# Other columns of the input projection emitted between the units of the second layer's recurrence

## The chip, the cores and the metric

One core of one Trainium2 chip runs the whole kernel in one launch. The metric is device time in microseconds. The kernel before took 1895.92 us, the median of three runs (1895.07, 1895.92 and 1908.12). All arithmetic is in float32. The large matrix products are done as three products each: both operands are split into a high part (float32r) and a low part, and high x high, high x low and low x high are added up in PSUM.

## The reference

Two layers act on 256 context tokens and 256 latent tokens of width 1024. Each layer starts with one input projection of the modulated stream, whose columns feed all branches:

```
p = modulate(x, shift, scale) @ w_in[l]
cq, ckv, kr, ch, cb, cc, rw, gt = split(p)
A) attention from cq, ckv, kr (low-rank, RMS norm, rotary key)
B) y = cb * conv3(cc * ch)
C) RWKV-7 from rw: features r, k, v, g, kk, decay, a, k_dir,
   then for each direction a scan over the tokens
   S = S*w - (S kk) (kk*a)^T + v k^T;   y = S r
   context first, the latent scan starts from the context's state
gates = sigmoid(gt)
o = (gates_A*(A @ w_o_attn) + gates_B*(B @ w_o_conv) + gates_C*(C @ w_o_rwkv)) @ w_out
x = layer_norm(alpha*x + g1*o)
x = layer_norm(alpha*x + g2*swiglu(modulate(x)))
```

In the second (last) layer only the latent tokens are wanted at the end. There the gates, the convolution, the queries and the read-out are computed for 256 tokens, while what the latent tokens read of the context (k, v, decay and the like, the key and value compression) is computed for 512.

## The kernel before, in words

**Columns.** `w_in` is padded and cut into 57 column blocks of 128 features. One block is `gemm_in` (line 426): 8 steps over the width with three matmuls each (`mm3`, lines 238 to 240), 24 matmuls into one PSUM bank of the pool `psg`, which has two. A block's weights come through a ring of four `hi` and four `lo` buffers of 512 columns, two of each to a block. They are split from the raw weight by ScalarE (`hi`, line 193) and by VectorE or POOL (`lo`, line 194), or, for 35 blocks of layer 1, they have been split during layer 0's FFN, stored in DRAM, and are read back by four DMAs (`wready`, line 209). Those 35 are all recurrence features that are loaded this way, the six compressed blocks, four gates and the twelve convolution blocks. The other 20 gates are split on the spot.

**What is made of a block.** A recurrence feature (`feature`, line 463) is mixed with its neighbours in time and stored to DRAM. A compressed block (line 548) is stored, and its squares are summed by four or two small matmuls (line 559). A gate (line 572) goes through a tanh and is stored. A convolution (`conv`, line 578) takes three blocks. All of them use one tag of four staging buffers (`stage`). Between gates and convolutions `mod_step` computes pieces of the next modulation, one step at a time (line 259).

**Recurrence.** `rwkv_half` (line 947) is a generator that runs once for the context half and once for the latent half of the tokens. Up to its first `yield` it makes eight units, one for each pair of heads and each direction: `stage1` (features, decay, cumulated sums) and `stage2` (products in chunks of 64 into `AR` and `LB`), with `stage1` one unit ahead. After the `yield` it inverts the triangular blocks: 31 steps on VectorE (lines 1085 to 1097), then small matmuls (lines 1110 and 1122). Last comes the scan, four chunks in each direction (lines 1154 to 1213). The latent half of layer 1 also reads out (`y`), and stores the result at line 1215.

**Order.** In layer 1 the program emits: the features except `late_f` (r for four blocks and the output gate's feature), both parts of the context half, the five `late_f`, both parts of the latent half, the six compressed blocks and their inverse norms, four gates, four convolutions, twenty gates. The framework sorts this at build time: each instruction has the rank of its place in the program, and each engine is given, along a simulated time line, the lowest-ranked of those that are ready. On the chip each engine, and SP's DMA queue, then runs its list in order.

**After the mixer.** Attention follows (lines 662 to 770): it loads the compressed blocks, normalizes them with `rsd` (lines 675 to 688) into `ch` and `cl`, and makes v, k and q. `qT` and `kT` are allocated in the space of `xh` and `xl`, the modulated stream that `gemm_in` reads (line 699). `rwkv_tail` (line 1217) finishes the read-out.

Of the kernel before, what the change touches and what calls it, by code (L numbers as in the profile page):

```python
# [12 lines left out]
ALU = mybir.AluOpType  # L13
# [5 lines left out]
T = 512  # L19
HT = 256  # L20
# [4 lines left out]
C = 64  # L25
# [3 lines left out]
RMS_EPS = 1e-6  # L29
# [31 lines left out]
CONV_AT = (20, 4)  # L61
# [7 lines left out]
VB = 1  # L69
# [2 lines left out]

N_AHEAD = 35
AHEAD_W13, AHEAD_W2 = 1.0, 1.0


@with_exitstack
def body(ctx: ExitStack, tc: tile.TileContext, A: dict, out: bass.AP, dbg=None, upto=None):
# [250 lines left out]
    def pow_mhalf(out_, in_, n):  # L329
        e = mhalf[0:out_.shape[0]]  # L330
        for _ in out_.shape[2:]:
            e = e.unsqueeze(2)
        e = e.to_broadcast(list(out_.shape))
        pool.tensor_tensor(out=out_, in0=in_, in1=e, op=ALU.pow)  # L334
# [98 lines left out]
    def seg(a):  # L433
        return a.rearrange("p (s t) -> p s t", t=HT)

    def layer(l, xh=None, xl=None, pre=()):
# [16 lines left out]
        with ExitStack() as rws:  # L453
# [5 lines left out]
            def rt(name, shape, dt=F32, bufs=1):  # L459
                return rp.tile(shape, dt, tag=name, name=name, bufs=bufs)  # L460
# [52 lines left out]
            def feat_gemm(m):  # L513
                feature(m, pre[m - R_K] if 0 <= m - R_K < len(pre) else gemm_in(l, M_RW + m, xh, xl, HT if m in late_f else 0, T))
# [12 lines left out]
                if n == (n0 if last else n0 + 2):  # L527
                    rnT = norms_t(nst["rn"], rt)

            S = [None, None]  # L530
            for z in range(2):
                S[z] = rt(f"S{z}", [128, 4, C])
                pool.memset(S[z], 0.0)
            for half in range(2):
                g = rwkv_half(l, half, last, rt, S, rnT)
                next(g)
                if l == 0 and half == 0:
                    for m in range(R_V, R_GD):
                        v = rt("vin", [128, 2, HT], bufs=VB)
                        sp.dma_start(out=v, in_=seg(feat_d[l][m]))  # L540
                        by_token(m, v, rt("vou", [128, T], bufs=VB))
                next(g, None)
                if half == 0:
                    for m in late_f:
                        feat_gemm(m)


            for i in range(6):
                a = s0 if i < 3 else 0
                ps = gemm_in(l, M_CQ + i, xh, xl, a * HT, T)  # L550
                t = stage("cqs")
                act.copy(out=t[:, a:2, 0:HT], in_=seg(ps)[:, a:2])
                sp.dma_start(out=seg(cq_d[l][i])[:, a:2], in_=t[:, a:2, 0:HT])
                if i < 5:
                    sq = stage("sqs")
                    act.activation(out=sq[:, a:2, 0:HT], in_=t[:, a:2, 0:HT], func=ACTF.Square)
                    pst = pg()
                    for tt in range(2 * a, 4):
                        pe.matmul(pst[:, tt:tt + 1], sq[:, tt // 2, (tt % 2) * 128:(tt % 2 + 1) * 128], ones[:, 0:1],
                                  start=(tt == 2 * a), stop=True, skip_group_check=True)  # L560
                    act.copy(out=ssq[:, i, 2 * a:4], in_=pst[:, 2 * a:4])

            o = q0 // 128
            for i, c, n in ((0, 0, 384), (3, 4, 256)):
                k = o if i == 0 else 0
                r = rsd[:, c + k:c + 4]
                dve.tensor_tensor(out=r, in0=ssq[:, i, k:4], in1=ssq[:, i + 1, k:4], op=ALU.add)
                if i == 0:
                    dve.tensor_tensor(out=r, in0=r, in1=ssq[:, 2, k:4], op=ALU.add)
                dve.tensor_scalar(out=r, in0=r, scalar1=1.0 / n, scalar2=RMS_EPS, op0=ALU.mult, op1=ALU.add)  # L570
            pow_mhalf(rsd[:, o:8], rsd[:, o:8], 8 - o)
            def gate(i):
                ps = gemm_in(l, M_GT + i, xh, xl, q0, T)
                gt = stage("gt")
# [19 lines left out]
                sp.dma_start(out=seg(br_d[l][1][i])[:, s0:2], in_=h_)  # L594


            n = 0
            for i in list(range(8, 24)) + list(range(8)):
                if n == CONV_AT[l]:
                    for k in range(4):  # L600
                        conv(k)
                gate(i)
                if n < N_EARLY[l]:
                    mod_step()
                n += 1
            if CONV_AT[l] > 23:
                for k in range(4):
                    conv(k)
            mod_step(100)
        if upto == "rwkv":  # L610
            mix.close()
# [332 lines left out]
        dve.tensor_copy(out=rnT, in_=prt)  # L944
        return rnT

    def rwkv_half(l, half, last, rt, S, rnT):
        read = not (last and half == 0)
        h0 = half * HT
        ncol = 128 if read else 64  # L950
# [123 lines left out]
        for n, u in enumerate(units):  # L1074
            cur = nxt
            if n + 1 < len(units):
                nxt = stage1(*units[n + 1])
            stage2(*u, *cur)

        yield  # L1080

# [313 lines left out]
```

## Time and profile before

| | |
|---|---|
| median of three runs | 1895.92 us |
| profiled execution | 1895.05 us |
| its span, first to last instruction | 1893.3 us |
| mean granted TensorE clock | 0.972 of full speed |
| TensorE busy, matmuls | 1811.6 us (96%) |
| TensorE busy, weight loads | 1480.6 us (78%) |
| VectorE, ScalarE, POOL busy | 1101.3, 830.8, 584.0 us |
| DMA | 374.16 MB, mean 198 GB/s |

The profiled execution lies 0.9 us under the median. Busy times of engines overlap, so they don't add up to the span. A matmul's busy time contains the time in which it flows through the array, while the next is already issued. PEclk is the clock that was granted to TensorE, as a share of 2.4 GHz. Layer 0 ends and layer 1 begins at about 1160 us; layer 1's mixer runs to about 1680.

### The profile page before, as it was taken

The numbers are of one execution on the slowest core, as the hardware profiler recorded it, in microseconds if no ns is written. First come the engines' busy times: TensorE is split into PE (matmuls) and PEld (weight loads), VectorE is DVE, ScalarE is ACT, GpSimd is POOL, SyncE is SP. The second block draws the span as 40 slices with busy tenths as digits, with TensorE's granted clock in tenths as the row PEclk, the third lists the DMA queues.
The fourth block names the chain that finished last, engine by engine and source line by source line (L and its number), as shares of the span: only waits on it lengthen the run. The fifth ranks groups of instructions, "written<-read, shape, count | busy, mean of one in ns | idle before, by whom it ended". The sixth has DMA issues, their size and how long they took to land. (4 is left out here: it accounts for less than half of the span.)

```text
span 1893.3 us, 35504 instructions
## 1 busy us (share of the span) xinstructions
PE 1811.6 (96%) x13556; PEld 1480.6 (78%) x13556; DVE 1101.3 (58%) x2066; ACT 830.8 (44%) x1798; POOL 584.0 (31%) x626
## 2 busy tenths in 40 slices
PE   7999999999989999999999998999999999989997
PEld 5787767777768767877788887877788896869996
DVE  4358724883357778642444337166974368875665
ACT  2556333733235453443454212275433364535552
POOL 1468113811124214534341005365412132320001
PEclk9999999999989999999999999998899999979999
DMA  8443544344485326699997323776586573576563
GB/s 338 134 142 98 171 132 132 113 156 135 142 300 174 120 69 230 221 370 340 338 343 286 135 97 138 244 221 191 172 264 227 175 264 114 177 248 223 188 233 114
DMA packets 180971, 374.16 MB, mean 198 GB/s; under 512 B 33792, under 2 KB 89152, under 8 KB 180800
## 3 DMA queue, kind: packets, MB, share of 16 engines
q1 hardware_dynamic: 177824, 363.30, 57.0%
q10 hardware_dynamic: 2976, 8.59, 1.3%
q8 instruction: 107, 1.75, 0.4%
q14 instruction: 64, 0.52, 0.1%
HBM read 298.39 MB, written 73.43 MB: 196 GB/s over the span
## 5 line engine op out<-in xcount | busy, mean ns | idle before, releaser
L194 DVE TENSOR_TENSOR lo<-raw,hi 128x512 fp32r<-128x512 f32 (+1 forms) x408 | 314.4, 781 | 320.1 <-ACT hi L193 305.9
L193 ACT CAST hi<-raw 128x512 fp32r<-128x512 f32 x478 | 286.8, 616 | 401.8 <-PE p_f L239 97.6
L238 PE MATMUL pg<-xh,hi 128*128 128x512 f32 (+1 forms) x912 | 334.8, 369 | 6.9 <-ACT pp L468 2.7
L239 PE MATMUL pg<-xl,hi 128*128 128x512 f32 (+1 forms) x912 | 330.3, 362 | 1.3 <-DVE xl L246 1.3
L240 PE MATMUL pg<-xh,lo 128*128 128x512 f32 (+1 forms) x912 | 328.7, 361 | 0.7 <-DMA lo<-win 0.6
L238 PE MATMUL p_f<-x2h,hi 128*128 128x256 f32 (+1 forms) x688 | 232.4, 338 | 6.5 <-ACT hi L193 4.2
L239 PE MATMUL p_f<-x2l,hi 128*128 128x256 f32 (+1 forms) x688 | 231.5, 337 | 0.3 <-DVE x2l L246 0.3
L240 PE MATMUL p_f<-x2h,lo 128*128 128x256 f32 (+1 forms) x688 | 231.3, 337 | 0.4
L238 PEld LDWEIGHTS pg<-xh,hi 128*128 128x128 f32 x912 | 178.7, 197 | 40.9 <-issue 7.8
L239 PEld LDWEIGHTS pg<-xl,hi 128*128 128x128 f32 x912 | 179.6, 197 | 25.8 <-issue 2.1
L240 PEld LDWEIGHTS pg<-xh,lo 128*128 128x128 f32 x912 | 179.5, 197 | 25.0 <-issue 1.3
L194 POOL TENSOR_TENSOR lo<-raw,hi 128x512 fp32r<-128x512 f32 x70 | 92.6, 1324 | 301.9 <-ACT hi L193 272.1
L238 PEld LDWEIGHTS p_f<-x2h,hi 128*128 128x128 f32 x688 | 131.2, 191 | 21.4 <-ACT hi L193 5.6
L240 PEld LDWEIGHTS p_f<-x2h,lo 128*128 128x128 f32 x688 | 131.2, 191 | 15.8 <-DVE lo L194 2.2
L239 PEld LDWEIGHTS p_f<-x2l,hi 128*128 128x128 f32 x688 | 131.3, 191 | 13.3 <-DVE x2l L246 0.6
L231 POOL TENSOR_TENSOR wlo<-wraw,whi 128x512 fp32r<-128x512 f32 x70 | 93.6, 1359 | 141.3 <-ACT whi L230 141.3
L334 POOL TENSOR_TENSOR rs<-rs,mhalf 128x1 f32<-128x1 f32 x12 | 9.4, 780 | 350.2 <-DVE rs L353 350.2
L1213 POOL TENSOR_TENSOR S<-S,PC 128x256 f32<-128x256 f32 x28 | 17.9, 640 | 152.1 <-DVE SV L1212 128.6
L651 POOL TENSOR_TENSOR acc<-acc,gts 128x512 f32<-128x512 f32 (+1 forms) x32 | 38.4, 1208 | 78.2 <-DVE gts L649 58.5
L864 DVE TENSOR_TENSOR su<-su,p_f 128x256 f32<-128x256 f32 (+1 forms) x43 | 23.7, 550 | 66.0 <-PE p_f L240 65.9
L1038 POOL TENSOR_TENSOR FM<-ta,di 64x256 f32<-64x256 f32 x64 | 53.3, 833 | 17.3 <-ACT FM L1032 7.4
L259 PE MATMUL pg<-raw,cs 128*32 128x128 f32 x1024 | 54.4, 306 | 3.9 <-DMA raw<-in_modw_dram 2.9
(392 smaller groups left out, 3715.3 us busy)
## 6 DMA issues: line engine op xcount, KB each, us to landing
raw<-in_modw_dram SPq DMA_DIRECT2D x96, 512.0 KB, 5.0
raw<-in_w_dram SPq DMA_DIRECT2D x88, 512.0 KB, 4.6
raw<-in_win_dram SPq DMA_DIRECT2D x79, 512.0 KB, 4.3
raw<-in_ffn_w_dram SPq DMA_DIRECT2D x44, 512.0 KB, 4.2
wraw<-in_win_dram SPq DMA_DIRECT2D x35, 512.0 KB, 7.0
win<-whi SPq DMA_DIRECT2D x35, 512.0 KB, 6.3
win<-wlo SPq DMA_DIRECT2D x35, 512.0 KB, 6.1
hi<-win SPq DMA_DIRECT2D x70, 256.0 KB, 3.6
```

What stands on the lines that cost most here:

```text
L193: act.copy(out=hi, in_=r)
L194: e.tensor_tensor(out=lo, in0=r, in1=hi.bitcast(F32), op=ALU.subtract)
L231: pool.tensor_tensor(out=lo[:, s], in0=raw[:, s], in1=hi[:, s].bitcast(F32), op=ALU.subtract)
L238: pe.matmul(ps, wh, xh, start=first, stop=False, skip_group_check=True)
L239: pe.matmul(ps, wh, xl, start=False, stop=False, skip_group_check=True)
L240: pe.matmul(ps, wl, xh, start=False, stop=last, skip_group_check=True)
L259: pe.matmul(ps[32 * (k % 4):32 * (k % 4) + 32, 0:128], cs[:, o:o + 32], raw[:, k], start=(j == 0 and k < 4), stop=(k >= 4), skip_group_che ...
L334: pool.tensor_tensor(out=out_, in0=in_, in1=e, op=ALU.pow)
L651: pool.tensor_tensor(out=a, in0=a, in1=g, op=ALU.add)
L864: dve.tensor_tensor(out=su[:, q0:T], in0=su[:, q0:T], in1=pw[1][:, q0:T], op=ALU.mult)
L1038: pool.tensor_tensor(out=FM[r, :, k0:k0 + 64], in0=rc(ta[r]), in1=rc(Pi[r]), op=ALU.mult)
L1213: pool.tensor_tensor(out=S[z], in0=S[z], in1=pc, op=ALU.mult)
```

## The change

What follows the recurrence in a layer's program (the compressed blocks, the inverse norms, the gates with their modulation steps, and the convolutions) is put into a list `rest`, each entry with a weight: the number of 256-token blocks in it, 0 for norms and modulation steps. In layer 1 the five `late_f` features head the list. `rwkv_half` gets a function `fill` and calls it after each unit's `stage2`. It takes entries off the list until weight 2 is used up (a remainder is carried over). What is left after both halves is emitted then, in the old order. `FILL = (0, 2)`: in layer 0 nothing is taken between units. No computation is added or removed.

```diff
+FILL = (0, 2)
...
-            for half in range(2):
-                g = rwkv_half(l, half, last, rt, S, rnT)
-                next(g)
...
-                next(g, None)
-                if half == 0:
-                    for m in late_f:
-                        feat_gemm(m)
-            for i in range(6):
+            def compressed(i):
...
-            n = 0
-            for i in list(range(8, 24)) + list(range(8)):
+            rest = [(2 - s0 if i < 3 else 2, lambda i=i: compressed(i)) for i in range(6)] + [(0, inverse_norms)]
+            convs = [(3 * (2 - s0), lambda i=i: conv(i)) for i in range(4)]
+            for n, i in enumerate(list(range(8, 24)) + list(range(8))):
                 if n == CONV_AT[l]:
-                    for k in range(4):
-                        conv(k)
-                gate(i)
+                    rest += convs
+                rest.append((2 - s0, lambda i=i: gate(i)))
                 if n < N_EARLY[l]:
-                    mod_step()
-                n += 1
+                    rest.append((0, mod_step))
+            due = [0]
+
+            def fill(n):
+                due[0] += n
+                while rest and due[0] >= rest[0][0] > 0 or n and rest and rest[0][0] == 0:
+                    w, f = rest.pop(0)
+                    due[0] -= w
+                    f()
...
+            rest = [(1, lambda m=m: feat_gemm(m)) for m in late_f] + rest
+            for half in range(2):
+                g = rwkv_half(l, half, last, rt, S, rnT, lambda: fill(FILL[l]))
+                next(g)
...
+                next(g, None)
+            fill(1000)
             mod_step(100)
...
             stage2(*u, *cur)
+            fill()
```

## Rows read from the trace of the kernel before

**Rows 1.** The page: engines (busy us, share, instructions), and one group of part 5.
```profile
PE 1811.6 (96%) x13556; PEld 1480.6 (78%) x13556; DVE 1101.3 (58%) x2066; ACT 830.8 (44%) x1798; POOL 584.0 (31%) x626
...
L259 PE MATMUL pg<-raw,cs 128*32 128x128 f32 x1024 | 54.4, 306 | 3.9 <-DMA raw<-in_modw_dram 2.9
```
**Rows 2.** Windows: stretch, length, PE, PEld, DVE, ACT, POOL busy, PEclk, DMA share, GB/s.
```profile
1226.00:1303.00 77.00, 74.91 (x469) 61.90 (x468) 43.37 (x80) 53.09 (x147) 46.09 (x69) 0.91 0.71 214
1303.00:1388.00 85.00, 79.27 (x749) 66.00 (x750) 73.00 (x141) 45.05 (x117) 36.99 (x51) 0.90 0.56 179
1388.00:1430.00 42.00, 41.39 (x571) 36.59 (x570) 36.99 (x98) 8.06 (x22) 4.52 (x8) 1.00 0.92 297
1430.00:1503.00 73.00, 72.30 (x1214) 61.55 (x1212) 25.50 (x52) 25.13 (x54) 14.80 (x20) 1.00 0.53 171
1503.00:1552.00 49.00, 48.21 (x415) 47.19 (x415) 34.06 (x62) 27.97 (x59) 16.46 (x14) 1.00 0.89 299
1552.00:1640.00 88.00, 82.87 (x563) 65.16 (x561) 67.11 (x155) 45.90 (x109) 25.25 (x29) 0.98 0.41 128
```
**Rows 3.** Tiles of the movable blocks, layer 1: ns min/median/max, first to last start.
```profile
L468 ACT COPY pp<-pg x15: 372/585/595, 1181.0 to 1273.0; 128x512 f32<-128x512 f32 x10, 128x256 f32<-128x256 f32 x5
...
L552 ACT COPY cqs<-pg x6: 372/474/588, 1281.8 to 1349.5; 128x256 f32<-128x256 f32 x3, 128x512 f32<-128x512 f32 x3
...
L575 ACT ACTIVATE gt<-pg x24: 372/378/392, 1355.7 to 1551.9; 128x256 f32<-128x256 f32 x24
...
L589 DVE SCALAR_TENSOR_TENSOR hs<-u,sv,hs x8: 401/481/1034, 1394.9 to 1449.3; 128x256 f32<-128x256 f32 x8
L582 ACT COPY hs<-pg x4: 372/373/380, 1388.9 to 1442.2; 128x256 f32<-128x256 f32 x4
L586 DVE TENSOR_TENSOR u<-pg,hs x4: 423/425/425, 1393.8 to 1447.1; 128x256 f32<-128x256 f32 x4
```
**Rows 4.** Tiles of the recurrence, layer 1, LBa (context) and LB (latent).
```profile
L1185 PE MATMUL p_c<-Zs,LBa x128: 218/218/268, 1384.0 to 1428.7; 64*64 64x64 f32 x128
L1056 ACT COPY LBa<-p_G x16: 344/362/364, 1247.6 to 1302.9; 32x256 f32<-32x256 f32 x16
...
L1085 DVE STREAM_TRANSPOSE sq<-LBa x1: 1976/1976/1976, 1303.9 to 1303.9; 128x1024 f32<-128x1024 f32 x1
...
L1192 PE MATMUL p_y<-LB,SV x128: 217/218/268, 1453.1 to 1502.8; 64*64 64x64 f32 x128
L1056 ACT COPY LB<-p_G x16: 344/362/366, 1307.5 to 1383.1; 32x256 f32<-32x256 f32 x16
...
L1085 DVE STREAM_TRANSPOSE sq<-LB x1: 1942/1942/1942, 1385.5 to 1385.5; 128x1024 f32<-128x1024 f32 x1
```
**Rows 5.** Windows of line 240 alone (8 of 24 matmuls per block): PE, PEld.
```profile
1388.00:1430.00 42.00, 17.93 (x62) 11.58 (x61) 1.00 0.92 297
1430.00:1503.00 73.00, 22.74 (x77) 14.39 (x76) 1.00 0.53 171
```
**Rows 6.** Timeline of TensorE among the last gates: start, us, what.
```profile
1543.01 0.28 PE L240 MATMUL pg<-xh,lo 128*128 128x256 f32 x1
1543.13 0.28 PE L238 MATMUL pg<-xh,hi 128*128 128x256 f32 x1
```
**Rows 7.** Timeline of SP and VectorE behind the latent scan.
```profile
1503.46 0.33 SPq L1215 DMA_DIRECT2D yf<-sq  x1
...
1510.10 0.48 DVE L686 SCALAR_TENSOR_TENSOR cqs<-cqs,sv,p_G 128x256 f32<-128x256 f32 x1 [1.21 <-DMA cqs<-cq]
...
1512.02 0.41 DVE L246 TENSOR_TENSOR cl<-cqs,ch 128x256 fp32r<-128x256 f32 x1
```
**Rows 8.** Groups of VectorE by line, 1503 to 1552: busy us, mean ns, idle before.
```profile
L194 DVE TENSOR_TENSOR lo<-raw,hi 128x512 fp32r<-128x512 f32 x21 | 15.4, 737 | 6.5 <-ACT hi L193 6.3
```
**Rows 9.** Waits of the SP queue, 1230 to 1390: us in total, times, longest.
```profile
SPq L209 <- PE pg L240: 51.8, 26, 7.1
```
**Rows 10.** DMA issues, 1226 to 1388: count, KB each, median us to landing.
```profile
hi<-win SPq DMA_DIRECT2D x34, 256.0 KB, 3.4
```

More of the change, by code (lines that the diff above doesn't have):

```diff
@@ L528, in layer @@
                     rnT = norms_t(nst["rn"], rt)
[L530 to L533, printed above, removed]
-            for half in range(2):
-                g = rwkv_half(l, half, last, rt, S, rnT)
-                next(g)
[L537 to L541, printed above, removed]
-                next(g, None)
-                if half == 0:
-                    for m in late_f:
-                        feat_gemm(m)
-            for i in range(6):
+            def compressed(i):
                 a = s0 if i < 3 else 0
@@ L561, in layer, with inverse_norms @@
                     act.copy(out=ssq[:, i, 2 * a:4], in_=pst[:, 2 * a:4])
[L563 to L571, printed above, removed]
+            def inverse_norms():
+                o = q0 // 128
+                for i, c, n in ((0, 0, 384), (3, 4, 256)):
+                    k = o if i == 0 else 0
+                    r = rsd[:, c + k:c + 4]
+                    dve.tensor_tensor(out=r, in0=ssq[:, i, k:4], in1=ssq[:, i + 1, k:4], op=ALU.add)
+                    if i == 0:
+                        dve.tensor_tensor(out=r, in0=r, in1=ssq[:, 2, k:4], op=ALU.add)
+                    dve.tensor_scalar(out=r, in0=r, scalar1=1.0 / n, scalar2=RMS_EPS, op0=ALU.mult, op1=ALU.add)
+                pow_mhalf(rsd[:, o:8], rsd[:, o:8], 8 - o)
             def gate(i):
@@ L594, in conv @@
                 sp.dma_start(out=seg(br_d[l][1][i])[:, s0:2], in_=h_)
-            n = 0
-            for i in list(range(8, 24)) + list(range(8)):
+            rest = [(2 - s0 if i < 3 else 2, lambda i=i: compressed(i)) for i in range(6)] + [(0, inverse_norms)]
+            convs = [(3 * (2 - s0), lambda i=i: conv(i)) for i in range(4)]
+            for n, i in enumerate(list(range(8, 24)) + list(range(8))):
                 if n == CONV_AT[l]:
-                    for k in range(4):
-                        conv(k)
-                gate(i)
+                    rest += convs
+                rest.append((2 - s0, lambda i=i: gate(i)))
                 if n < N_EARLY[l]:
-                    mod_step()
-                n += 1
-            if CONV_AT[l] > 23:
-                for k in range(4):
-                    conv(k)
+                    rest.append((0, mod_step))
+            rest += convs if CONV_AT[l] > 23 else []
+            due = [0]
[5 more added lines that the diff above has]
+                    f()
+            S = [None, None]
+            for z in range(2):
+                S[z] = rt(f"S{z}", [128, 4, C])
+                pool.memset(S[z], 0.0)
+            rest = [(1, lambda m=m: feat_gemm(m)) for m in late_f] + rest
+            for half in range(2):
+                g = rwkv_half(l, half, last, rt, S, rnT, lambda: fill(FILL[l]))
+                next(g)
+                if l == 0 and half == 0:
+                    for m in range(R_V, R_GD):
+                        v = rt("vin", [128, 2, HT], bufs=VB)
+                        sp.dma_start(out=v, in_=seg(feat_d[l][m]))
+                        by_token(m, v, rt("vou", [128, T], bufs=VB))
+                next(g, None)
+            fill(1000)
             mod_step(100)
@@ L945, in norms_t, with rwkv_half @@
         return rnT
-    def rwkv_half(l, half, last, rt, S, rnT):
+    def rwkv_half(l, half, last, rt, S, rnT, fill):
         read = not (last and half == 0)
```

## The prediction

> **What bounds the kernel now.** I read the page's engine line first [rows 1]: TensorE is busy 96% of the span, but its weight loads (PEld) only 78%. A matmul's busy time runs on while the next one already streams, so the first figure can't say how much room is left, and the second is the one to follow. Layer 0 is emitted as before: with a fill of 0, nothing leaves the new list until both recurrences are out, and the list has the old order. So only the second layer's mixer, about 1174 to 1640, can change.
>
> Next, the table of its stages [rows 2], with the recurrence's tiles, which name the borders [rows 4]. Five stretches matter:
> - U0, 1226 to 1303: the eight units of the context half (first `LBa` writes, to 1302.9).
> - U1, 1303 to 1388: the eight units of the latent half (`LB` to 1383.1), while VectorE inverts the context half's blocks (from 1303.9).
> - C, 1388 to 1430: inversion of the latent half (from 1385.5) beside the context scan (1384.0 to 1428.7).
> - R, 1430 to 1503: solving steps and the latent scan (last `LB` product 1502.8).
> - E, 1503 to 1552: gates alone.
>
> The reader should see three things. E is dense: PEld 47.19 of 49 us. U0 and U1 are not: 61.90 of 77 (80%) and 66.00 of 85 (78%), at a granted clock of 0.91 and 0.90, where C, R and E have 1.00. As the clock has two levels (1.2 and 2.4 GHz), 0.91 and 0.90 mean 14 and 17 us at the lower. And attention, which follows (1552 to 1640), is not TensorE's stage: PEld 65 of 88, VectorE 67 of 88. Its q and k tiles take the space of `xh` and `xl`, which every gate reads, so the last gate (1551.9) opens it.
>
> The third view is when the movable columns run now [rows 3]. Emitted behind everything, they are already pulled forward: late features to 1273.0, compressed columns 1281.8 to 1349.5, the first gates at 1355.7, convs from 1388.9. The order on the engines is planned at build time by readiness, and the place in the program is a rank in it, not a position. So the change raises ranks; it does not open a gap that was empty.
>
> **The change, part by part.**
> Counts. A fill of 2 per unit is 32 in weight over 16 units: 5 late features (5), 3 + 3 compressed (9), 4 gates, 4 convs (12), 2 gates. 18 gates keep the last place. Ahead of the last unit the old order has run the features, the compressed columns and 4 gates; new there are 12 conv columns and 2 gates, 14 columns of 256 tokens.
>
> Cost in U0 and U1. A column is 24 matmuls at 0.12 us start to start [rows 6], 2.9 us; 14 make 40 us. What room takes them? At the share that C reaches with recurrence and columns mixed (36.59 of 42, 87%), U0 and U1 have 77 x 0.067 + 85 x 0.095 = 13 us; at E's 96% they have 28. The 31 us at the lower level cost at most half, 15 us; I take half of that back, 8, as denser stretches hold 1.00. So the units end 40 - 13 - 8 = 19 us later; the ends are 0 (28 + 15 cover it all) and 40 (no room). I take 13 and not 28 because C is the nearest row that mixes both kinds.
>
> By busy matmul time there would be almost no room in U0 (74.91 of 77) and 6 us in U1: the delay would be some 32 us and the sum below about +2. The Trainium skill ("Perfetto Trace Analysis", Identifying the Most-Contended Engine) says that matmul occupancy is no measure of headroom and weight-load occupancy is. The trace agrees in E, where both are at 96% or more, and I follow PEld.
>
> What comes with the columns: VectorE gets four convs of 0.42 + 2 x 0.48 + 0.42 = 1.8 us (line 593 has the shape of line 586) [rows 3], 7 us, beside 73.00 busy of 85 in U1, which fits; ScalarE has 40 us free there. SP issues four loads per pre-split column; now 1226 to 1388 holds 17 of them (34 high halves) [rows 10], and from 1230 to 1390 SP stood 51.8 us waiting for a ring buffer that a matmul had not released [rows 9], with the units' own feature loads queued behind. 12 more columns add 12 MB over 162 us, 74 GB/s on 214 and 179, under the 299 of E. I cost the queue at nothing, covered by one unit's lead of stage 1; if that cover goes it is 51.8 x 12/17 = 37 us, which belongs to the slow rival. Modulation steps ride with gates and convs: 10 of 16 go ahead of the last unit where 4 had; a step is 8 matmuls, 54.4 / 128 = 0.4 us [rows 1], so six more cost 2.6 us at most and nothing where TensorE waits anyway; I take nothing.
>
> What leaves E. C and R together carry (62 + 77) / 8 = 17.4 columns now (the third matmul of each of a column's eight steps) [rows 5]; they would have 18 gates to carry. So one gate, 2 us, is left behind the scan, and E gives back 47 us. At R's rate in both (77/8 over 73 us) they carry 15, and E gives back 41. The gates split their weights on ScalarE, VectorE and POOL, 0.74 us a half on VectorE [rows 8], where convs loaded theirs split but had 1.8 us of products each, so C's VectorE (36.99 of 42) is no worse off. I take 47.
>
> What E covered. After the last store of the scan (1503.46) the normalized inputs of attention need 6.6 us to the first product and 8.6 to the first low half [rows 7]; gates hide this now. With one gate left, TensorE stands for about 8 us (ends 0 and 15, the latter if all five low halves are waited for). And VectorE's work of E other than splits, 34.06 - 15.4 = 19 us [rows 2, 8], the readout's tail above all, moves into attention, whose VectorE has 21 us free: between 0 and 19, I take 9.
>
> Sum: -47 + 19 + 8 + 9 = **-11 us**. The profiled execution took 1895.05 us (span 1893.3), 0.9 under the median of 1895.92, so the forecast is 1884.
>
> **The rivals.**
> *Room fully used.* With more columns beside each unit the clock stays up and PEld nears E's share: delay 0 to 10, and -47 + 5 + 8 + 9 = -25, 1870. For it: from 1226 to 1552 the clock falls in the units alone, never in C, R or E [rows 2]. Against: U1 is also VectorE's (86%), and fuller TensorE does not shorten that.
>
> *The recurrence is pushed back.* This one ends slower. The place is the in-order queues of SP and TensorE in U0 and U1: fill columns now rank above the next unit, a feature load waits behind weight loads that wait for ring buffers, and the chain unit, inversion, scan slips by the whole 40 us. The scan then ends late with no dense work left to cover attention's start: -47 + 40 + 15 + 13 = +21, 1916. It decides once the units slip by more than 47 - 17 = 30 us. For it: SP's 51.8 us of waiting, and that before the change the unit always went first. Against: a unit takes some 10 us and two columns take 5.8, so both fit in a unit's time.
>
> *The rank hardly matters.* The plan already fills by readiness [rows 3]; TensorE's work is the same, and what leaves E comes back in the units: 40 us in, 40 to 47 out, the cover lost at the end: 1895, give or take 4.
>
> **How the numbers follow.** Forecast (3 to 19 us gained) 0.40; room fully used 0.27; rank hardly matters 0.16; pushed back 0.17. A measurement here tells 1%, 19 us, from no change: under 1877 or over 1915. Faster by that: the second case and a tail of the first, 0.30; slower: most of the last, 0.15; within: 0.55. All ends added give 1848 to 1928; leaving about a tenth on either side, the range is 1856 to 1912; the forecast's own is 1876 to 1892.
>
> **What would show it.** Layer 0 and the features to about 1220 unmoved. First conv product before 1340 instead of 1394. Units ending near 1405, PEld there at 87%, granted clock above 0.95. Scan end near 1522, one or two gates after it, then a gap of some 8 us on TensorE before the first product on `ch`, and attention a little longer than 88 us. I am wrong if the units end after 1418, if gates still run 30 us past the scan (the order did not move, or C and R carry less), or if attention grows by more than 19 us.

## The result: slower by one per cent, and the profile after

The changed kernel took 1917.59 us (median of 6 executions, 1911.18 to 1931.68), the kernel before 1899.36 us beside it (6 executions): a ratio of 1.0104, 95% interval 1.0057 to 1.0152. The forecast was 1884 us with a range of 1856 to 1912; the sign was wrong and the median lies above the range.

The profiled execution took 1914.15 us, 19.1 more than that of before, at a mean clock of 0.970 where before had 0.972. The page's engine line, to be held against [rows 1]:

```profile
span 1912.3 us, 35508 instructions
...
PE 1809.8 (95%) x13556; PEld 1481.8 (77%) x13556; DVE 1104.4 (58%) x2066; ACT 832.2 (44%) x1798; POOL 589.0 (31%) x626
```

The same matmuls, busy for the same time, in a span 19 us longer: work has only moved. The layer began 4.6 us earlier in this execution (first `pp` evacuation at 1176.4, before at 1181.0 [rows 3]), while TensorE's order is the same up to 1242 us. So whoever compares absolute times adds 4.6 us to those of after. Code lines move by 2 early in the file, by 9 or 10 late (L240 to L242, L1056 to L1065, L1192 to L1202).

The tiles of the movable columns and of the recurrence come next (ns min/median/max, first to last start), to be held against [rows 3, 4]:

```profile
L470 ACT COPY pp<-pg x15: 363/586/593, 1176.4 to 1263.3; 128x512 f32<-128x512 f32 x10, 128x256 f32<-128x256 f32 x5
L537 ACT COPY cqs<-pg x6: 356/481/587, 1266.1 to 1313.8; 128x256 f32<-128x256 f32 x3, 128x512 f32<-128x512 f32 x3
L563 ACT ACTIVATE gt<-pg x24: 363/380/392, 1319.8 to 1547.3; 128x256 f32<-128x256 f32 x24
L574 DVE TENSOR_TENSOR u<-pg,hs x4: 402/412/425, 1356.4 to 1425.5; 128x256 f32<-128x256 f32 x4
L1065 ACT COPY LBa<-p_G x16: 345/362/365, 1241.1 to 1316.3; 32x256 f32<-32x256 f32 x16
L1195 PE MATMUL p_c<-Zs,LBa x128: 218/218/267, 1397.2 to 1442.6; 64*64 64x64 f32 x128
L1065 ACT COPY LB<-p_G x16: 345/363/365, 1333.9 to 1419.1; 32x256 f32<-32x256 f32 x16
L1202 PE MATMUL p_y<-LB,SV x128: 218/218/267, 1497.9 to 1548.9; 64*64 64x64 f32 x128
```

The reader should see three things, all with the 4.6 us added. The last compressed column and the first gate come 31 us earlier than before, the first conv product 33 us earlier: the ranks did what they say. The context units end 18 us later (1316.3 against 1302.9), the latent ones 40.6 us later (1419.1 against 1383.1), the scan 50.7 us later (1548.9 against 1502.8). And the last gate has not moved at all: 1547.3 + 4.6 is 1551.9, the time of before. It used to run 49 us behind the scan; now the two end together.

The windows of the same stretches show what this did to the density (length, PE, PEld, DVE, ACT, POOL busy, PEclk, DMA share, GB/s; to be held against [rows 2]). The borders are those of after: context units, latent units, latent inversion, solving and latent scan, attention.

```profile
1221.00:1316.00 95.00, 91.02 (x554) 76.25 (x553) 42.03 (x74) 52.09 (x141) 38.91 (x60) 0.91 0.72 215
1316.00:1421.00 105.00, 97.93 (x1117) 85.26 (x1117) 85.60 (x169) 52.58 (x136) 47.27 (x67) 0.93 0.75 239
1421.00:1471.00 50.00, 44.91 (x542) 39.42 (x540) 43.56 (x98) 15.28 (x35) 12.30 (x14) 0.97 0.69 211
1471.00:1549.00 78.00, 75.28 (x1164) 67.13 (x1162) 29.19 (x56) 35.75 (x73) 17.55 (x17) 0.98 0.47 144
1552.00:1663.00 111.00, 96.62 (x636) 77.40 (x637) 85.43 (x196) 56.76 (x131) 36.08 (x37) 0.95 0.47 149
...
1553.00:1563.00 10.00, 5.96 (x17) 4.62 (x18) 6.61 (x15) 2.85 (x6) 0.18 (x1) 0.50 0.92 299
```

PEld was 80% and 78% of the units' stretches before; it is 80% and 81% now. The clock was 0.91 and 0.90; it is 0.91 and 0.93. Columns were put in, and the stretches did not become denser: they became longer, 77 to 95 and 85 to 105 us. The matmuls of one line alone in the context units say by how much (busy us, mean ns, idle before). First before, 1226 to 1303:

```profile
L240 PE MATMUL pg<-xh,lo 128*128 128x256 f32 x62 | 19.9, 321 | 0.0
L240 PE MATMUL pg<-xh,lo 128*128 128x512 f32 x9 | 3.5, 389 | 0.0
```

The same line after, 1221 to 1316:

```profile
L242 PE MATMUL pg<-xh,lo 128*128 128x256 f32 x64 | 19.9, 311 | 0.0
L242 PE MATMUL pg<-xh,lo 128*128 128x512 f32 x33 | 13.8, 418 | 0.0
```

Each block has eight such matmuls, so three 512-token columns (24 more matmuls) came in, the latent half's compressed columns. A 512-token matmul costs 0.23 us start to start, as the timeline of after shows in one of these columns (seven steps in 1.59 us):

```profile
1289.72 0.39 PE L241 MATMUL pg<-xl,hi 128*128 128x512 f32 x1
...
1291.31 0.39 PE L242 MATMUL pg<-xh,lo 128*128 128x512 f32 x1
```

Three columns of 24 are 16.3 us, the few more 256-token matmuls about 1.5: 18 us of columns for 18 us of delay. There was no room.

**The account of TensorE.** I counted the column matmuls in each stretch of both traces, at 0.12 us [rows 6] and 0.227 us start to start; what is left of a stretch is the recurrence's small matmuls, other work and waiting. Stretches as in the prediction, their borders at the ends of the last instructions that name them (us):

| stretch | before: length = columns + rest | after: length = columns + rest |
|---|---|---|
| U0, context units | 77.3 = 27.8 + 49.5 | 95.4 = 45.8 + 49.6 |
| U1, latent units | 80.2 = 29.3 + 50.9 | 102.7 = 39.4 + 63.4 |
| C, latent inversion | 47.6 = 24.2 + 23.3 | 52.6 = 25.9 + 26.7 |
| R, solving, latent scan | 71.7 = 26.8 + 44.9 | 76.7 = 37.4 + 39.3 |
| E, gates alone | 49.0 = 40.4 + 8.5 | 0 |
| together | 325.8 = 148.5 + 177.1 | 327.4 = 148.5 + 179.0 |

The 40.4 us of columns that left E stand, to the tenth, in the four stretches ahead: 18.0 + 10.1 + 1.7 + 10.6. So 14 columns left E, but only some ten of them (28.1 us) stand ahead of the last unit; the other four run in C and R. In U1 the rest grew by 12.5 as well: the context half's inversion and scan now run inside it (about 240 small matmuls more there, as many fewer in C and R together), because the latent units take longer, and so do 64 more matmuls of modulation steps. TensorE's list is nearly full from the first unit to the last gate: matmuls are busy in all but 10 of 326 us before [rows 2] and all but 19 of 328 after, by the windows. So an order in which nothing is left behind the scan is one in which the scan ends last.

That alone would be no loss: 327.4 against 325.8. The loss comes behind it. Attention with its merges, from the later of scan end and last gate to the last merge matmul, took 102.2 us before and takes 121.4. The timeline behind the scan (start, us, what; idle before and its releaser in brackets):

```profile
1547.97 1.14 PE L1202 MATMUL p_y<-LB,SV 64*64 64x64 f32 x16 [0.52 <-ACT SV L1196]
...
1550.44 3.12 SPq L684 DMA_DIRECT2D cqs<-cq  x5
...
1554.58 0.48 DVE L695 SCALAR_TENSOR_TENSOR cqs<-cqs,sv,p_G 128x256 f32<-128x256 f32 x1 [3.73 <-DMA cqs<-cq]
...
1555.31 1.38 PE L689 MATMUL p_G<-dg,ones 128*128 128x128 f32 x4 [3.91 <-DVE dg L688]
...
1558.42 0.79 PE L240 MATMUL pg<-hi,ch 128*128 128x512 f32 x1 [1.73 <-ACT ch L247]
```

Between 1549.1, when the last matmul of the scan ends, and 1558.4 TensorE has a dozen small matmuls and nothing else: the compressed blocks are loaded, normalized, split. Before, gates stood over this work [rows 7]. The granted clock then drops to its lower level for about 10 us, seen in the row of 1553:1563 above as 0.50, after a stretch in which TensorE had done little. The balance of the profiled pair: last merge matmul +21.0 us after the layer's start (1.8 of list, 19.2 of attention), +2.8 behind it, -4.6 from the earlier start, which makes 19.2; the spans differ by 19.0.

### The profile page after: what moved, and what is told of

The parts are those of the page before. It is cut to its first block, busy times and chain, and to the rows that moved or that the text cites. A ratio compares the mean times of both kernels' runs of the same rounds, so it can differ in the third digit from the quotient of the medians.

```text
span 1912.3 us, 35508 instructions
## 1 busy us (share of the span) xinstructions
PE 1809.8 (95%) x13556; PEld 1481.8 (77%) x13556; DVE 1104.4 (58%) x2066; ACT 832.2 (44%) x1798; POOL 589.0 (31%) x626
## 5 line engine op out<-in xcount | busy, mean ns | idle before, releaser
L240 PE MATMUL pg<-xh,hi 128*128 128x512 f32 (+1 forms) x912 | 334.6, 368 | 11.0 <-ACT pp L470 2.8
L242 PE MATMUL pg<-xh,lo 128*128 128x512 f32 (+1 forms) x912 | 328.6, 361 | 0.0
L240 PE MATMUL p_f<-x2h,hi 128*128 128x256 f32 (+1 forms) x688 | 233.1, 339 | 5.2 <-ACT hi L195 5.2
L242 PE MATMUL p_f<-x2h,lo 128*128 128x256 f32 (+1 forms) x688 | 231.9, 338 | 2.8 <-DVE lo L196 2.4
L240 PEld LDWEIGHTS pg<-xh,hi 128*128 128x128 f32 x912 | 179.2, 197 | 44.5 <-issue 6.3
L242 PEld LDWEIGHTS pg<-xh,lo 128*128 128x128 f32 x912 | 179.2, 197 | 25.0 <-issue 2.3
L240 PEld LDWEIGHTS p_f<-x2h,hi 128*128 128x128 f32 x688 | 131.9, 192 | 19.9 <-ACT hi L195 6.4
L242 PEld LDWEIGHTS p_f<-x2h,lo 128*128 128x128 f32 x688 | 131.8, 192 | 18.2 <-DVE lo L196 5.1
```

Of the source, the lines that this page charges most:

```text
L240: pe.matmul(ps, wh, xh, start=first, stop=False, skip_group_check=True)
L242: pe.matmul(ps, wl, xh, start=False, stop=last, skip_group_check=True)
```

## Experiments

Each of the four groups of runs stands beside the kernel before on the same chip: 1897.45, 1896.47, 1896.72 and 1896.86 us, in the order below except that the modulation kernel belongs to the third. Places in the schedule are those of one profiled execution of each kernel. They count from the layer's first `pp` evacuation, so that a clock that differs earlier in the program plays no part; a clock that differs within the layer still does. In the expectations, W is the theory that TensorE's list has no room; Q and S put the loss down to queues and ranks, or to the ring of weight buffers.

### Is it TensorE's work, SP's queue, or the mere place in the order?

Two pairs, each made on the order of before (b) and that of after (a). First, columns that are half as long:

```diff
-        for k in range(8):
-            mm3(..., k == 0, k == 7)
+        ks = range(8) if l == 0 or M_RW <= m < M_CH else range(4)
+        for k in ks:
+            mm3(..., k == 0, k == ks[-1])
```

> The kernel before with the same half of the matmuls left out: some 60 us of TensorE work less (24 gates, 12 convolution and 6 compressed blocks at 12 matmuls). W: the dense gates behind the scan shrink or vanish (49 us before), so this one is faster than before by 40 to 60 us, and the cut changed kernel by as much or more, since attention then starts uncovered in both; the two differ by under 10 us. Q: the difference between the two stays at 18 us or grows.

> The changed kernel with half of the matmuls of the second layer's compressed blocks, gates and convolutions left out (steps 0 to 3 of 8; their outputs are partial sums), loads and evacuations as they are. Read against the same cut in the kernel before. Theory W (TensorE's list had no room: each moved column costs its own time in the units): with half the cost the units and the scan slip by about half, the latent scan ends some 20 to 25 us later than in the cut kernel before, instead of 51. Theory Q (the slip comes from the queues and ranks: loads that wait for ring buffers, evacuations ahead of the next unit): the work per column on SP, ScalarE and VectorE is the same, so the scan still ends 45 to 50 us later.

b_thin took 1877.39 us (ratio 0.9891, 0.9858 to 0.9923), a_thin 1887.12 (0.9926, 0.9883 to 0.9969). The scan ended at 347.5 us in b_thin and at 337.8 in a_thin: not 20 to 50 us later, but 10 us earlier. Neither number came, and for a reason nobody had put down: with half of the columns' matmuls gone TensorE ran at its lower clock for 119 us (b_thin) and 85 us (a_thin) between the layer's start and the last gate, where before has 34. The profiled execution of b_thin (1894.03 us) is also 17 us longer than its median. b_thin ran 34 us longer at the lower level, which at half speed costs 17 us at most; with those taken off, a_thin's scan would end some 7 us the later. What does follow: with columns half as long the changed order holds the recurrence up little, so a place in the order that delays a unit by 45 us and more, whatever the size of what is put ahead of it, is refuted. The medians of the pair still differ by 9.7 us against the change, but less at equal clock: executions at 0.948 took 1894.03 us in b_thin and 1889.12 and 1893.22 in a_thin, at 0.955 it was 1873.04 and 1880.44 against 1880.94, at 0.959 to 0.960 1875.12 against 1881.45.

Second, columns that load nothing, their weights taken from the resident `xh` and `xl`:

```diff
-        wh, wl = wready(m) if l and m in win_d else wload(...)
+        if l and not M_RW <= m < M_CH:
+            wh, wl = (lambda k, t=t: t[:, k, 0:128] for t in (xh, xl))
+        else:
+            wh, wl = wready(m) if l and m in win_d else wload(...)
```

> The kernel before with the same loads and splits left out. W: total within 10 us of the uncut kernel, since TensorE bounds these stages; the pair keeps its difference of 15 to 20 us. S: gains some 10 to 20 us in the units, and the changed kernel gains more, so the pair's difference goes to zero or turns round.

> The changed kernel where the second layer's compressed blocks, gates and convolutions use a slice of the resident input as weights (their outputs are not the reference's): no weight loads and no splits for them, all matmuls and evacuations kept. W: TensorE's work is the same, so the latent scan still ends 40 to 50 us later than in the kernel before with the same cut. Theory S (the ring of weight buffers and SP's queue hold the units up): without these loads the units slip by 0 to 15 us, and the kernel gains 30 us or more on the uncut one.

b_noload took 1898.5 us (1.0014, 0.998 to 1.0049), a_noload 1908.92 (1.0052, 1.0004 to 1.0100). The waits of SP's queue for a weight buffer that a matmul holds (us in total, times, longest) were these in after, 1222 to 1421:

```profile
SPq L211 <- PE pg L242: 51.1, 33, 4.5
SPq L211 <- PE pg L241: 15.4, 4, 7.6
```

and in a_noload, 1222 to 1430:

```profile
SPq L1082 <- ACT tms L1080: 35.0, 8, 10.8
...
SPq L211 <- PE pg L242: 14.0, 9, 2.1
```

The waits on which the slow rival rested fall from 66.5 us to 14, and the queue now stands mostly for the store of a unit's own product (`tms`), that is, behind the units. The scan is still 38 us later than in the other half of the pair (355.7 against 317.7), and the latent units 44.6 (243.9 against 199.3), as the tiles say; b_noload, then a_noload:

```profile
L1059 ACT COPY LB<-p_G x16: 345/363/367, 1304.7 to 1380.8; 32x256 f32<-32x256 f32 x16
```

```profile
L1068 ACT COPY LB<-p_G x16: 345/362/366, 1339.0 to 1429.4; 32x256 f32<-32x256 f32 x16
```

So the loads are not what delays the chain. With them gone the pair differs by 10.4 us, not 18. That doesn't show that the rest of the loss hangs on the loads: b_noload's own attention is 10 us longer than that of before, for a reason that the section on attention gives.

### Which part of the fill does it?

Half the weight (`FILL = (0, 1)`), the fill in the context half alone, and in the latent half alone, with `late_f` between the halves as before:

```diff
-FILL = (0, 2)
+FILL = (0, 1)
```

```diff
-                g = rwkv_half(l, half, last, rt, S, rnT, lambda: fill(FILL[l]))
+                g = rwkv_half(l, half, last, rt, S, rnT, lambda: fill(FILL[l] if half == 0 else 0))
```

```diff
-            rest = [(1, lambda m=m: feat_gemm(m)) for m in late_f] + rest
...
-                g = rwkv_half(l, half, last, rt, S, rnT, lambda: fill(FILL[l]))
+                g = rwkv_half(l, half, last, rt, S, rnT, lambda: fill(FILL[l] if half == 1 else 0))
...
+                if half == 0:
+                    for m in late_f:
+                        feat_gemm(m)
```

> The changed kernel with a fill of 1 per unit instead of 2: ahead of the last unit 5 late features, 6 compressed blocks and 2 gates have a rank, no more columns than the old order ran there by readiness (5, 6 and 4 gates). W: the units slip by 0 to 10 us, a row of dense gates of 25 us or more stays behind the scan and covers attention's start, total within 8 us of before. Q (ranks above the next unit hold the units up): about half of the slip of the fill of 2, scan 20 to 25 us later, total 8 to 12 us over before.

> The changed kernel with the fill in the context half alone (5 late features, 6 compressed blocks, 2 gates); everything else behind both halves. W: the first eight units end about 18 us later as with the full change (their added columns are the same), the latent half then has fewer columns left to carry and gives most of it back by running them by readiness; scan 5 to 25 us later, 8 or more gates behind it, total within 8 us of before. Q: the context half's slip stays (18 us) to the end, total 10 us or more over before.

> The changed kernel with the fill in the latent half alone (6 compressed blocks, 4 gates, 1 convolution); late features between the halves as before. W: three columns more than the old order ran there, so the units end some 9 us later, 30 us of gates stay behind the scan, total within 8 us of before. Q: the latent half's part of the slip (22 us of 40) shows, total 10 us or more over before.

| | time, us | ratio, 95% | U0 ends | U1 ends | scan ends | last gate | gates behind the scan |
|---|---|---|---|---|---|---|---|
| before | 1896.47 | | 122.5 | 202.7 | 322.0 | 370.9 | 15 |
| fill1 | 1900.61 | 1.0018, 0.9996 to 1.0041 | 128.0 | 208.5 | 334.9 | 380.3 | 13 |
| half1 | 1898.13 | 1.0015, 0.9984 to 1.0045 | 128.7 | 207.5 | 328.5 | 381.1 | 15 |
| half0 | 1908.80 | 1.0076, 1.0050 to 1.0103 | 136.9 | 225.2 | 352.0 | 364.0 | 4 |
| after | 1917.59 | 1.0104, 1.0057 to 1.0152 | 140.6 | 243.4 | 372.7 | 370.9 | 0 |

Times are medians of 10 executions (before 25; after 6, beside another 1899.36 of before). The profiled executions took 1905.69 us (fill1), 1904.27 (half1) and 1898.84 (half0, the shortest of its ten), with 51, 51 and 24 us at the lower clock ahead of the last gate, where before has 34; a few us in the columns of places are this. The gates and the scan of half0, as its tiles give them:

```profile
L563 ACT ACTIVATE gt<-pg x24: 364/380/391, 1315.0 to 1539.2; 128x256 f32<-128x256 f32 x24
...
L1202 PE MATMUL p_y<-LB,SV x128: 218/218/268, 1474.9 to 1526.9; 64*64 64x64 f32 x128
```

Half of the weight per unit, and the fill in the latent half alone, change nothing: the order planned by readiness comes out almost as before, with 13 and 15 gates behind the scan. These two bear out the rival that the rank hardly matters, for their size of change. The context half alone makes most of the loss. There the three 512-token columns go ahead of the last context units, and what follows is drawn forward by readiness, although nothing ranks it higher in the latent half: the first matmul columns of three of the four convolutions stand ahead of the end of the last latent unit in half0, none in before. Theory W had expected a scan 5 to 25 us later, 8 gates or more behind it and a total within 8 us; it was 30 us, 4 gates and 12 us, so its numbers failed here, and the 10 us or more of theory Q came. Counted as in the account above, though, 29.6 us of columns moved ahead of half0's scan (10.8 stand behind it, before 40.4), and the scan ends 30.0 us later: what W had too low is how many columns readiness draws forward, not what a column costs. The nearer the scan's end comes to the last gate, the slower the kernel.

### Is there room in the units at all, and what is the cover worth?

One extra column of 24 matmuls behind each of the 16 units, on resident operands, with no load and no evacuation, in the order of before:

```diff
             stage2(*u, *cur)
+            if last:
+                extra_column[0]()
```

> The kernel before with one extra column of 24 matmuls (2.9 us) behind each of the 16 units, on resident operands: no load, no split, no evacuation, result unused; 46 us of TensorE work beside the units and nothing else. Theory W (no room in TensorE's list): the scan ends later by some 40 to 50 us, the last gate too, since all its work is kept, and as the gates still stand behind the scan the total grows by 40 to 46 us. The forecast's theory (room of 13 to 28 us by weight-load share, 8 to 15 by the clock): total grows by 5 to 25 us.

b_extra took 1951.52 us (two executions; 1.0287, 1.0232 to 1.0342), 54.8 more than before. The columns are 16 x 24 x 0.12 = 46 us. They find no room anywhere. The chain itself slips by 8 us only (scan end 330.1 against 322.0), not by the 40 to 50 expected, since the extra columns displace others: no gate stands ahead of the last latent unit, where before has four, and 20 stand behind the scan. So the run shows that the list as a whole has no room; of the units alone it says less. The tiles of b_extra show the gates running 100 us past it:

```profile
L582 ACT ACTIVATE gt<-pg x24: 367/379/391, 1427.7 to 1607.2; 128x256 f32<-128x256 f32 x24
L1201 PE MATMUL p_y<-LB,SV x128: 218/218/267, 1454.3 to 1507.0; 64*64 64x64 f32 x128
```

Next, 15 of the 24 gates left out, in both orders:

```diff
             def gate(i):
+                if last and i not in range(8, 17):
+                    return
...
+                if last and i == 9:
+                    for o in list(range(17, 24)) + list(range(8)):
+                        sp.dma_start(out=seg(gate_d[l][o])[:, s0:2], in_=gt[:, s0:2, 0:HT])
```

> The kernel before with the last 15 gates of the second layer left out (their places are filled with another gate's values): the dense stretch behind the scan is gone, about 45 us of TensorE work and its weight loads. Cover theory: attention now starts uncovered, as with the change, and takes 115 to 122 us from the end of the scan instead of 102 from the last gate, so the total falls by 25 to 35 us and not by 45 to 49. If the cover is worth nothing (attention was long in the changed kernel for another reason), the total falls by 45 or more.

> The changed kernel with the same 15 gates left out; there they run beside the inversion and the scan. W: the order no longer matters where so little is left; units as in the changed kernel, 18 columns less in the stretches behind them, which shorten by 10 to 30 us; total within 10 us of the cut kernel before plus the columns that stand ahead of its scan, so 0 to 25 us over it. If the chain of inversion and scan bounds these stretches by its own latency and the gates were free there: the total falls by under 8 us.

b_cut took 1874.38 us (two executions; 0.9880, 0.9828 to 0.9932), a_cut 1886.67 (0.9939, 0.9907 to 0.9971). The scan and the last merge of b_cut:

```profile
L1197 PE MATMUL p_y<-LB,SV x128: 218/218/268, 1457.2 to 1503.9; 64*64 64x64 f32 x128
...
L238 PE MATMUL pg<-bra,hi x32: 278/281/389, 1611.3 to 1633.1; 128*128 128x256 f32 x32
```

In b_cut the chain runs as in before (scan end 319.7 against 322.0), and nothing runs behind it: 49 us of stretch E are gone, and the kernel gains 22. Attention with its merges takes 129 us instead of 102, with 20 us of it at the lower clock. The price of the uncovered start is 27 us there, more than I had for it. It is more than the 19 of the change because SP issues the loads of the compressed blocks (`cqs`) at 1512.2, 8 us after the scan, where in after they come 1.3 us after it; the first product on `ch` is 6 us later for that. In a_cut the latent units still end 54 us later than in b_cut (257.1 against 203.0), while C and R, which have only five columns left to carry, take 88 us instead of 117; the scan ends 25.6 us later and the pair differs by 12.3 us. C and R together, a_cut:

```profile
1440.60:1528.80 88.20, 65.49 (x1264) 57.04 (x1262) 53.23 (x123) 24.75 (x56) 15.57 (x19) 0.83 0.40 123
```

and b_cut:

```profile
1387.50:1504.20 116.70, 115.27 (x1874) 99.67 (x1872) 65.34 (x155) 33.11 (x75) 18.05 (x29) 1.00 0.68 217
```

This pair shows where the account ends. Both kernels have the same columns, 105.3 us, ahead of the scan's end, and a_cut needs 25.6 us more for them: with its columns used up in the units, TensorE's matmuls are busy for 65.5 of the 88.2 us, at a clock of 0.83, while the inversion and the scan set the time. Columns beside that chain fill holes which columns in the units don't have. Part of the 25.6 is clock: the profiled execution of a_cut took 1895.29 us, 9 over its median.

### What makes attention longer?

Three things had moved into it: TensorE's bare start, the lower clock, and the read-out's tail on VectorE. First, the order of before with the modulation steps taken out of the gates and emitted in attention's loop:

```diff
-N_EARLY = (24, 24)
-N_CONV = (2, 1)
+N_EARLY = (24, 0)
+N_CONV = (2, 0)
...
-            mod_step(100)
+            if not last:
+                mod_step(100)
...
+                    if last:
+                        mod_step(2)
```

> A try at a faster kernel, from the kernel before: the 16 modulation steps of the second layer's mixer are emitted inside the attention loop, two behind each pair of heads, instead of behind gates and convolutions. If TensorE is full up to the last gate and has holes in attention, the last gate comes 8 to 14 us earlier, attention stays as long, and the total falls by 5 to 12 us. If attention's TensorE list is full in the same sense, or its waits grow by the steps' loads, no change or slower.

b_modlate took 1915.35 us (1.0093, 1.0062 to 1.0124). The last gate came 9.4 us earlier (361.5 against 370.9), and attention took 133 us instead of 102. The idea was that attention has room on TensorE for these small matmuls; it did not find any. Matmuls were busy for 117.9 of the 133 us, before for 96.2 of 102.1, so attention had 22 us more of them and 9 us more without any; why that is more than the steps' own 14 us (256 matmuls in the trace, at 54.4/1024 us each [rows 1]) is open. An expected gain became a loss as large as that of the change itself.

Then the tail left out of the second layer, in both orders:

```diff
     def rwkv_tail(...):
...
+        if l == NL - 1:
+            for hp in range(4):
+                sp.dma_start(out=br_d[l][2][hp][:, h0:h0 + HT], in_=Yf[:, hp])
+            return
```

> The kernel before with the same tail left out, which mostly runs beside the gates behind the scan: the total falls by 0 to 6 us, and from the last gate to the last merge matmul it still takes 96 to 102 us. It is the base for the cut changed kernel.

> The changed kernel with the second layer's read-out tail left out (normalization, bonus and gate; the scan's result is passed on as it is). In the changed kernel attention, with the merges, took 121 us from the end of the scan to the last merge matmul, where before it took 102 from the last gate. If the 19 us are the bare start of attention alone, this kernel and the cut kernel before still differ by 17 to 19 us there. If the tail's VectorE work, now inside attention, is part of it, the difference falls to 9 to 13 us.

b_notail took 1891.85 us (0.9976, 0.9939 to 1.0012), a_notail 1913.86 (1.0089, 1.0057 to 1.0120): the loss is still there, 22 us. The score matmuls and the last merge, in b_notail:

```profile
L745 PE MATMUL p_G<-kT,qT x32: 590/592/595, 1565.7 to 1614.5; 96*128 96x512 f32 x32
...
L238 PE MATMUL pg<-bra,hi x32: 277/281/384, 1631.6 to 1648.5; 128*128 128x256 f32 x32
```

and in a_notail:

```profile
L754 PE MATMUL p_G<-kT,qT x32: 590/592/595, 1596.4 to 1645.1; 96*128 96x512 f32 x32
...
L240 PE MATMUL pg<-bra,hi x32: 278/282/388, 1662.3 to 1678.0; 128*128 128x256 f32 x32
```

Without the tail, attention takes 99.7 and 115.3 us: 15.6 us apart, where with the tail it is 19.2. By that the tail's share is some 3.6 us, from one execution of each, where kernels with 45 us of cover and more differ by as much among themselves (99 to 102, below); the medians, 22.0 us apart, show no smaller loss without it. It does hold up the scores: they begin 51 us after the scan in after and 33 in a_notail, but much of that is made good by the end. The other 16 us are the start without cover: in both changed kernels the first product on `ch` starts 9.3 us after the scan, in both others 1.7 us before the last gate's evacuation ends, and that later start makes 11 of them. All kernels in one table, the cover being the time from scan end to last gate, attention the time from the later of the two to the last merge matmul:

| kernel | cover, us | attention, us |
|---|---|---|
| before, half1, fill1, b_notail, b_extra | 49, 53, 45, 46, 100 | 102, 101, 101, 100, 99 |
| half0, a_noload | 12, 5 | 115, 116 |
| after, a_notail | none | 121, 115 |
| b_cut, b_thin, a_thin, a_cut | none | 129, 122, 122, 121 |
| b_noload | 45 | 112 |
| b_modlate (modulation inside) | 28 | 133 |

With 45 us of cover attention takes 99 to 102, with little or none 115 to 129. b_noload has the gates, and yet 112. VectorE's line in its trace says why:

```profile
1545.28 1.15 DVE L682 TENSOR_SCALAR dg<-ident,rsd 128x128 f32<-128x128 f32 x2 [22.63 <-PE p_G L683]
```

VectorE stood idle for 22.6 us until four small matmuls of the norms were done. Their operands were ready at 1511.7, and TensorE's list has them at 1544.9, among the matmuls of the last gates. The last low half was ready at 1552.0, 6.5 us after the last gate; in before it is ready 28 us ahead of the last gate. In half0 too it comes 6.1 us behind its last gate. So gates cover attention's start only where the norms run beside them, and not behind them.

No kernel here was faster than before without leaving work out; fill1 and half1 are equal to it within their intervals.

## Why the prediction was wrong, step by step

- **What E gives back was right, where it goes was not.** 14 columns were to leave E; 14 did, 40.4 us, and E gave back 49 us where I had 47. But all 14 were to stand ahead of the last unit, and some ten did (28 us). So the full 40 us by which the units slipped is not the 14 columns without room that my outer end stood for; that the two agree is chance.
- **The room in the units is the step that failed.** I took 13 us of room from the weight loads' 80 and 78% against the 87% of C, and 8 us from a clock that would rise. Neither was there: with 28 us more columns in them the units' stretches kept 80 and 81% of weight loads and a clock of 0.91 and 0.93, and b_extra paid 55 us for 46 us of columns. For these stretches, in which small matmuls of the recurrence stand between columns, 80% of weight loads is what a full list looks like. The rule of the Trainium skill ("Perfetto Trace Analysis", Identifying the Most-Contended Engine), that headroom is judged by the occupancy of weight loads, or by the share of peak arithmetic (which I did not work out), agrees with E, where both figures are near the top, but not with U0 and U1. The busy time of matmuls (74.91 of 77 [rows 2]), which I weighed and set aside, would have given about +2 for the sum and was the better of the two here, though no row shows that it is so in general.
- **The delay was mis-sized, 19 against 51 us.** The units end 40.7 us later, the outer end of what I had allowed ("no room"), of which 28 are columns and 12.5 the context half's inversion and scan drawn into the latent units. C and R, which were to carry 17 columns in the time of before, carried 22, and added another 10. The modulation steps, which I took at nothing, are a small part: a step's 8 matmuls are 16 in the trace, so it takes 0.85 us and not 0.4, and four more steps ran ahead of the last unit, 3.4 us. Had I summed columns and rest over the whole time from the first unit to the last gate, as in the table above, it would have come out at once: hardly anything idles there, so what E gives back the chain must pay.
- **The cover was right in sum, wrong in its parts.** 8 us for the bare start and 9 for VectorE's tail make 17; 19.2 were measured, but by the pair without the tail about 16 are the start and 3.6 the tail, so that the sum came out near is luck. TensorE's standstill of some 9 us was foreseen; the lower clock behind it was not.
- **With the measured terms** the sum is -49 + 51 + 19 + 3 = +24 from the layer's start, and +19 in the profiled pair, whose layers began 4.6 us apart.
- **The rivals.** The slow one gave 1916 and its point of decision (units later by more than 30 us) was passed, but not by its mechanism: SP's waits did not do it (the pair without loads), nor the place as such (the thin pair). Its time was right by luck: its 40 us of slip were 28 us of columns and 12.5 of other work, and its sum is in effect the third rival's conservation of TensorE's work with the cover lost. That rival, at 1895, counted the same work in and out but took the lost cover for little more than the 7 us by which its two sides differ. The first rival, room fully used, failed outright: the units were to end 0 to 10 us later at a higher clock and share of weight loads, and ended 40.7 later with both as before.
- **What I had said would show me wrong** did: the units end at 1423.7 on the clock of before, against a limit of 1418, and attention grew by 19.2, against 19. The first conv product came at 1361.0 on that clock, not before 1340.

What is not settled: how the other 5 of the 16 us of the uncovered start divide between lower clock and later evacuations; what the tail costs, if more than nothing; and how much of a_cut's later scan is the chain and how much the clock.

## What to carry to other kernels

Before work is moved ahead of a dependent chain, add up the engine's list over the whole time from the first place to the last: if hardly anything idles between, an earlier place for one thing is a later end for another; and work that filled the chain's own holes is missed there, as in a_cut. Independent work behind a chain is not waste but cover, here worth 19 to 27 us for the stage that starts next; it should be left where the next stage has loads and norms to wait for, and the norms must be able to run beside it. An occupancy below that of a dense stretch shows room only if a run that adds work there does not get longer.

## What the runs showed of the hardware

Where TensorE work was left out, the granted clock came down, and part of the gain went with it. The thin kernels leave out about 64 us of matmuls (half of 39 columns of 2.9 us and three of 5.4) and gained 20 and 10 us, at mean clocks of about 0.955 and 0.951 over their executions, where those of before lie between 0.964 and 0.978. Some 20 us of what is missing are the lost cover (attention 122 us in both, 102 before); how the rest divides no run shows.

The mean clock also goes with most of the spread of one and the same kernel. Executions of before took from 1888.00 us at 0.978 to 1914.48 at 0.965; a straight line through all 78 that stand beside the experiments, on four chips, falls by 1.6 us for each 0.001 and leaves a fifth of the variance. The loss of the change is not of this kind: the six executions of after lie 13 to 19 us above that line, 16 in the mean. At 0.970, for example, before took 1900.87, 1901.71 and 1904.37 us, after 1914.15 and 1915.10.
